# Inverting and gating the sums of two softmaxes together, in a two-layer decoder trunk

## Chip, cores and metric

The kernel runs on one core of a Trainium2 chip. The metric is the device time of one execution, in microseconds; the median of three runs of the kernel before is 620.65 us (620.62 to 620.73). Engines: PE is TensorE (PEld its weight loads), DVE is VectorE, ACT is ScalarE, POOL is GpSimd, SP is SyncE, which issues the DMAs.

## The reference

Two layers work on x of 256 tokens by 1024 columns, in float32. Each has an attention part and an MLP, both between RMS norms.

The attention part projects the normed x to 2848 columns. Eight heads are *gated* (called nsa): each has a compressed, a selected and a window branch. With 256 tokens, all four blocks of 64 are selected and the window covers every earlier key, so the selected and the window branch are two causal softmaxes over different keys and values. Their outputs are added with a sigmoid gate per token, head and branch. Eight other heads are *forgetting* (called fox): one causal softmax each, with a learned decay added to the scores.

```python
g = jax.nn.sigmoid(gate_logits + gate_bias)
o = g[..., 0:1] * o_cmp + g[..., 1:2] * o_sel + g[..., 2:3] * o_win    # per gated head
p = softmax(q @ k.T * scale + cum_q - cum_k, causal)                   # per forgetting head
x = x + rms_norm(concat([o_nsa, o_fox]) @ w_out, g_post_mix)
x = x + rms_norm(square(relu(rms_norm(x, g_pre_mlp) @ w_up)) @ w_down, g_post_mlp)
```

## The kernel before

**Tiles.** Tokens are cut in two halves of 128 (t = 0, 1). Every weight tile (512 KB mostly) is loaded by SP into wraw and split on chip into a rounded high part whi (an ACT copy) and the rest wlo (a DVE subtraction); a product is three matmuls, high by high, high by low, low by high. Seven whi and seven wlo tiles and nine raw ones rotate.

**Who sets the order.** The code doesn't issue instructions. It records them in a `Recorder`, which then plans the order on every engine: `schedule` (line 303) is a list scheduler that knows a cost for each operation (`_cost`, line 453), a latency between engines (`_latency`, line 430) and how many buffers each tag has; among the instructions that are ready it takes the one with the lowest rank. `order` (line 288) plans once by the recorded order and then four times more with due times worked back from the plan for PE (`deadlines`, line 260), and keeps the plan that ends first. So a change in what is recorded can move instructions on all engines. On the chip each engine then runs its own list in order and waits on semaphores. All recorded instructions carry line 411 in the profile, so one goes by tile names there.

**The attention stage.** A list `flat` has 24 entries per layer: for each of four pairs of gated heads, par = 0, 1 and branch br = 1, 2; then, for each of four pairs of forgetting heads, par = 0, 1. The loop at line 1378 walks it as a pipeline, entry i in the step i: in step i it records the scaling of entry i - 1, the scores and exponentials of entry i, and the transposes of entry i - 2; three entries behind, where a group of heads is complete, the products with the values (`pv`, line 1283). Between these it records pieces of the projections and of the output projection (`fill`, line 1198), so that PE has other matmuls while a softmax is under way.

For one entry, with 384 score columns (128 for t = 0, 256 for t = 1):

- `scores` (line 1231): PE writes scores to PSUM; for each t, DVE adds mask or decay, stores minus the scaled scores to the tile pr and their minimum to st[:, t]; ACT takes the exponential in place and puts its sum into st[:, 2 + t]. Both branches of a gated head come from one set of score matmuls (`nsa_scores`), both heads of a forgetting pair from another (`fox_scores`).
- `scale` (line 1253): DVE inverts the two sums with one reciprocal and multiplies pr, for each t, by the inverse; for a gated branch the same instruction multiplies by the gate too, as a second scalar operand.
- `probs_T` (line 1264): PE transposes pr in three blocks to PSUM, ACT copies that to prT (or, for odd pairs of gated heads, to a larger tile prX).

There are three pr tiles, four st tiles (128x4) and six prT tiles.

**The end of the stage.** The outputs (oT) are multiplied by w_out into four PSUM accumulators, x for t = 0 and acc for t = 1; the last four row blocks need the forgetting heads (`out_last`, line 1418). Then, for each t, `sandwich` (line 727) squares and sums on ACT, makes the new normed rows mg on DVE, PE turns mg (`to_xT`, line 710), and ACT and DVE split the turned rows into high and low parts of xT, with which the MLP's matmuls start.

Of the kernel before, what the change touches and what calls it, by code (L numbers as in the profile page):

```python
# [20 lines left out]
AF = mybir.ActivationFunctionType  # L21
OP = mybir.AluOpType
PSUM = bass.MemoryType.PSUM

P = 128
# [32 lines left out]
SEGS = ((0, 128, 0), (128, 384, 1))  # L58
# [474 lines left out]
def trunk(nc, A, consts_in, out, sbp, pp, dram):  # L533
    def tile(shape, dtype, name, tag=None, bufs=1):
        return nc.tile(sbp[(tag or name) not in OPERANDS], shape, dtype, name, tag, bufs)

    def psum(tag):
        return nc.tile(pp, [P, 512], F32, tag, tag, {"acc": 2, "x": 2, "s": 3, "o": 1}[tag], psum=True)

    def small(shape, name, bufs=2):  # L540
        return tile(shape, F32, name=name, tag=name, bufs=bufs)
# [17 lines left out]
    for l in range(DEPTH):  # L559
        at = 0  # L560
        for c, (a, b) in enumerate(CHUNKS):
# [3 lines left out]
            for q, (k0, k1) in enumerate(parts_of(l, c)):  # L565
# [4 lines left out]
                if (c, q) in RIDES:  # L570
                    s, j = RIDES[c, q]
# [39 lines left out]
    for k in range(8):  # L611
        if k in (2, 3):
            f = both[:, k - 2]
        elif k < 2:
            f = tile([P, D], F32, name="first", tag="raw", bufs=RBUFS)
        else:
            f = tile([P, D], F32, name="first", tag=f"act{k % 2}", bufs=2)
        o = 0 if k else 8
        f = f[:, 0:o + NFIRST]
        a = 8 + k * NFIRST - o  # L620
# [19 lines left out]
    ps = psum("o")  # L640
# [13 lines left out]
    def load_gains(*rows):  # L654
        g = tile([P, 2, D], F32, name="gains", tag="gain")
        for i, (name, l) in enumerate(rows):
            nc.sync.dma_start(g[:, i, :], A[name][l].partition_broadcast(P))
        return [g[:, i, :] for i in range(2)]
# [141 lines left out]
    for l in range(DEPTH):  # L800
# [6 lines left out]
        par = {} if first else dict(zip(("smT", "bias", "w2"), params))  # L807
        kv_tok, kS, kW, q_tok, q_rot = ([None] * 2 for _ in range(5))
        vS, vW, fV, gate = ([None] * 2 for _ in range(4))
        gates = small([P, NT, 24], "gate")  # L810
        T = {}
# [238 lines left out]
        def forget_bias(pair):  # L1050

            b = tile([P, 2, 384], F32, name="bias", tag="raw", bufs=RBUFS)
            nc.sync.dma_start(b, T["cum"][2 * pair:2 * pair + 2, :].partition_broadcast(P))
            for o in (0, 2 * P):
                nc.gpsimd.affine_select(out=b[:, :, o:o + P], in_=b[:, :, o:o + P], pattern=[[0, 2], [-1, P]],
                                        compare_op=OP.is_ge, fill=NEG, base=0, channel_multiplier=1)
            T["fb", pair] = b
# [140 lines left out]
        def fill(n):  # L1198
            for _ in range(n):
                if step() in ("wait", "end"):  # L1200
                    return
# [6 lines left out]
        def fox_scores(pair):  # L1208

            ps = [psum("s") for _ in range(2)]  # L1210
            rows = [slice(par * HD, par * HD + HD) for par in range(2)]
            with nc.stretch():
                for o, n, q0 in ((0, 128, 0), (128, 256, 128)):
                    for par, h in enumerate(rows):
                        nc.tensor.matmul(ps[par][:, o:o + n], T["fqT"][h, pair, q0:q0 + P], T["fkT"][h, pair, 0:n],
                                         start=o == 0, stop=o > 0, skip_group_check=True)
            return [(x[:, 0:128], x[:, 128:384]) for x in ps]

        def nsa_scores(e):

            pair, par = e[1:3]
            g = pair // 2
            q = T["qS"][:, 2 * pair + par, :]
            ps = [psum("s"), psum("x")]
            for t, n in ((0, P), (1, S)):
                for j in range(2):
                    nc.tensor.matmul(ps[t][:, :2 * n].rearrange("p (b n) -> p b n", b=2), q[:, t * P:t * P + P],
                                     kx[j][:, g, :, 0:n], start=j == 0, stop=j == 1)
            return [(ps[0][:, br * P:br * P + P], ps[1][:, br * S:br * S + S]) for br in range(2)]

        def scores(e):
            kind, pair, par, br = e[:4]
            if kind == "fox":
                if par == 0:
                    T["sc"] = fox_scores(pair)
                ps = T["sc"][par]
            else:
                if br == 1:
                    T["sc"] = nsa_scores(e)
                ps = T["sc"][br - 1]  # L1240
            p = small([P, 384], "pr", 3)
            st = small([P, 4], "st", 4)
            for a, b, t in SEGS:
                nc.vector.tensor_tensor_reduce(
                    out=p[:, a:b], in0=ps[t], in1=T["fb", pair][:, par, a:b] if kind == "fox" else
                    cst[:, C_MASK + 256 - (b - a):C_MASK + 256], op0=OP.add, op1=OP.min,
                    scale=-0.125, scalar=3.0e38, accum_out=st[:, t:t + 1])
            for a, b, t in SEGS:
                nc.scalar.activation(p[:, a:b], p[:, a:b], AF.Exp, scale=-1.0, bias=st[:, t:t + 1],
                                     accum_out=st[:, 2 + t:3 + t])  # L1250
            return p, st

        def scale(e, p, st):
            kind, pair, par, br = e[:4]
            nc.vector.reciprocal(st[:, 2:4], st[:, 2:4])
            for a, b, t in SEGS:
                if kind == "fox":
                    nc.vector.tensor_scalar(p[:, a:b], p[:, a:b], st[:, 2 + t:3 + t], None, op0=OP.mult)
                else:
                    c = 3 * (2 * pair + par) + br  # L1260
                    nc.vector.tensor_scalar(p[:, a:b], p[:, a:b], st[:, 2 + t:3 + t], gate[t][:, c:c + 1],
                                            op0=OP.mult, op1=OP.mult)

        def probs_T(p, eng, e):
            ps = psum("s")
            with nc.stretch():
                for a in (0, 128, 256):
                    nc.tensor.transpose(ps[:, a:a + P], p[:, a:a + P], ident)
            kind, pair, par, br = e
            if kind == "nsa" and pair % 2:  # L1270

                if br == 1:
                    T["prX"] = tile([P, 4, S], F32, name="prX", tag=f"act{par}", bufs=2).rearrange("p b n -> p (b n)")
                pT = T["prX"][:, (br - 1) * 384:br * 384]
            else:
                pT = small([P, 384], "prT", 6)
            if eng:
                nc.scalar.activation(pT, ps[:, :384], AF.Copy)
            else:
                nc.vector.tensor_copy(pT, ps[:, :384])  # L1280
            return pT
# [87 lines left out]
        flat = [("nsa", pair, par, br) for pair in range(4) for par in range(2) for br in (1, 2)]  # L1369
# [4 lines left out]
        st = {}  # L1374
# [1 line left out]
        o = None  # L1376
        nc.lane = len(nc.ops)
        for i in range(len(flat) + 4):
            if 0 <= i - 1 < len(flat):
                scale(flat[i - 1], *st[i - 1])  # L1380
            if i < len(flat):
                if 14 <= i < 22 and i % 2 == 0:
                    forget_bias(i // 2 - 7)
                st[i] = scores(flat[i])
                if i == 15:
                    done.add("nsa")
                    g_post, g_pre2 = load_gains(("g_post_mix", l), ("g_pre_mlp", l))
            fill(1)
            if i in side:
                side[i]()  # L1390
                fill(1)
            if 0 <= i - 2 < len(flat):
                pTs[flat[i - 2]] = probs_T(st.pop(i - 2)[0], 1, flat[i - 2])
            fill(1)
            j = i - 3
            if 0 <= j < len(flat) and flat[j][2] == 1 and flat[j][3] != 1:
                kind, pair, par, br = flat[j]
                if pair % 2:
                    o = psum("o")
                    if br:  # L1400
                        nc.tensor.matmul(o, T["vbig"][:, pair // 2], T["pcT"][pair // 2], start=True, stop=False,
                                         skip_group_check=True)
                    cols = lambda q: [(q // 2) * HD] * 2 if br else [2 * q * HD, 2 * q * HD + HD]
                    pv(o, [[([pTs.pop((kind, q, x, b)) for x in range(2)], (fV, vS, vW)[b], cols(q))
                            for b in ((1, 2) if br else (0,))] for q in (pair - 1, pair)], not br)
                    o_evac(o, kind, pair)
            if i >= 12 or i % 2:
                fill(1)
# [207 lines left out]
```

## Time and profile before

| | |
|---|---|
| median of the runs | 620.65 us |
| the profiled execution | 620.53 us, of it 618.4 us in the span of the trace |
| mean granted TensorE clock | 0.997 |
| instructions in the trace | 9854 |
| ACT's exponentials of pr | 96 |
| the first scaling of pr starts, the last one | 62.2 us, 419.9 us |

The profile is of one execution. Busy shares are of the span. A row of the view of groups gives the engine, the operation, out<-in by tile names with shapes, a count, the busy time with the mean duration of one in ns, and then the engine's idle time just before them with what ended it. A row of the view in order of time gives start and length in us, and a count of merged instructions; start to start of neighbours is what an engine needs for one, since the end of an instruction overlaps with the next. A row of the view of waits gives who waited for whom, the total, the number of times and the longest.

### The profile page before, as it was taken

The page shows a single profiled execution, that of the slowest core. Times are in us where ns is not written, and L with a number is a line of the kernel's source. Part 1 is how long each engine was busy: PE and PEld are TensorE (multiplying, and loading weights), DVE is VectorE, ACT ScalarE, POOL GpSimd, SP SyncE. Part 2 cuts the span into 40 slices and gives each one's busy share as a digit, 9 for nine tenths or more (in the row PEclk, how much of TensorE's full clock was granted, in tenths as well). Part 3 has the DMA queues.
Part 4 walks back from the last instruction along what each step waited for, and adds up shares of the span by engine and source line. Part 5 has one row for each costly group of instructions (what it writes and reads, how often), then busy time and mean ns, then how long its engine had stood idle before and what let it go on. Part 6 is the DMA issues. An engine that isn't in the chain of part 4 may idle for free.

```text
span 618.4 us, 9854 instructions
## 1 busy us (share of the span) xinstructions
PE 611.0 (99%) x3494; PEld 514.6 (83%) x3494; DVE 465.3 (75%) x1021; ACT 388.9 (63%) x760; POOL 10.8 (2%) x20
## 2 busy tenths in 40 slices
PE   9999999999999999999999999999999999999995
PEld 7989987788888888888888888778888888888884
DVE  6889998689966567557598999886996575566534
ACT  7766788567655555545466769775776456456522
POOL 0001200000000000000000020000000000000000
PEclk9999999999999999999999999999999999999998
DMA  8996746519765565564346781653386665666001
GB/s 323 401 355 209 268 137 223 171 36 307 254 191 191 182 205 196 184 197 140 107 137 239 265 312 71 204 205 104 131 299 203 191 197 175 200 197 181 32 0 68
DMA packets 34817, 118.86 MB, mean 192 GB/s; under 512 B 4144, under 2 KB 4304, under 8 KB 34768
## 3 DMA queue, kind: packets, MB, share of 16 engines
q1 hardware_dynamic: 34768, 118.23, 57.5%
q8 instruction: 27, 0.44, 0.3%
q14 instruction: 22, 0.18, 0.1%
HBM read 117.15 MB, written 1.07 MB: 191 GB/s over the span
## 4 chain that ended last, share of the span: by engine, by line
PE 99%; DVE 0%; DVEq 0%; issue 0%; ACT 0%
PE s L411 35%; PE acc L411 31%; PE x L411 25%; PE o L411 7%; DVE x L411 0%; DVE m L411 0%; DVEq L1612 0%; DVE rsqrt L411 0%; ACT rl L411 0%
## 5 line engine op out<-in xcount | busy, mean ns | idle before, releaser
L411 DVE TENSOR_TENSOR wlo<-wraw,whi 128x1024 fp32r<-128x1024 f32 (+1 forms) x188 | 225.5, 1201 | 97.9 <-ACT whi L411 57.9
L411 ACT ACTIVATE whi<-wraw 128x1024 fp32r<-128x1024 f32 (+1 forms) x188 | 195.4, 1042 | 108.2 <-PE acc L411 72.9
L411 PE MATMUL s<-xT,whi 128*128 128x512 f32 x448 | 106.5, 390 | 0.0
L411 PEld LDWEIGHTS s<-xT,whi 128*128 128x128 f32 x448 | 83.4, 188 | 16.8
L411 PE MATMUL x<-whi,aT 128*128 128x512 f32 x256 | 88.6, 391 | 0.0
L411 PE MATMUL acc<-whi,aT 128*128 128x512 f32 x256 | 88.4, 390 | 0.0
L411 PEld LDWEIGHTS s<-xT,wlo 128*128 128x128 f32 x448 | 57.4, 191 | 2.2
L411 PE MATMUL s<-xT,wlo 128*128 128x256 f32 x448 | 58.1, 283 | 0.0
L411 PEld LDWEIGHTS acc<-whi,aT 128*128 128x128 f32 x256 | 48.0, 188 | 10.0
L411 PEld LDWEIGHTS x<-whi,aT 128*128 128x128 f32 x256 | 48.1, 188 | 9.6
L411 PE MATMUL x<-wlo,aT 128*128 128x512 f32 x128 | 50.0, 390 | 0.0
L411 PE MATMUL acc<-wlo,aT 128*128 128x512 f32 x128 | 49.9, 390 | 0.0
L411 ACT ACTIVATE pr<-pr,st 128x256 f32<-128x256 f32 (+1 forms) x96 | 42.8, 449 | 5.8 <-DVE st L411 5.5
L411 PE MATMUL acc<-xT,whi 128*128 128x256 f32 (+1 forms) x192 | 42.4, 324 | 0.0
L411 PE MATMUL acc<-whi,xT 128*128 128x512 f32 (+1 forms) x128 | 37.2, 354 | 0.0
L411 PE MATMUL x<-whi,xT 128*128 128x512 f32 x112 | 35.7, 395 | 0.1
L411 PEld LDWEIGHTS acc<-xT,whi 128*128 128x128 f32 x192 | 31.7, 190 | 3.3 <-issue 0.8
L411 ACT ACTIVATE h<-s 128x256 f32<-128x256 f32 x56 | 21.2, 378 | 16.0 <-PE s L411 16.0
L411 ACT ACTIVATE rl<-h 128x512 f32<-128x512 f32 x28 | 17.7, 633 | 18.0 <-DVE h L411 18.0
L411 PE MATMUL acc<-xT,wlo 128*128 128x256 f32 x128 | 28.6, 286 | 0.0
L411 ACT ACTIVATE rl<-x 128x512 f32<-128x512 f32 x24 | 14.6, 610 | 22.2 <-PE x L411 18.0
L411 PEld LDWEIGHTS acc<-wlo,aT 128*128 128x128 f32 x128 | 24.0, 188 | 5.0
(220 smaller groups left out, 963.6 us busy)
## 6 DMA issues: line engine op xcount, KB each, us to landing
wraw<-in_w_up_dram SPq DMA_DIRECT2D x64, 512.0 KB, 4.0
wraw<-in_w_down_dram SPq DMA_DIRECT2D x64, 512.0 KB, 3.7
wraw<-in_w_in_dram SPq DMA_DIRECT2D x36, 512.0 KB, 4.9
wraw<-in_w_out_dram SPq DMA_DIRECT2D x16, 512.0 KB, 5.6
w<-in_cmp_w_k_dram SPq DMA_DIRECT2D x8, 512.0 KB, 4.9
w<-in_cmp_w_v_dram SPq DMA_DIRECT2D x8, 512.0 KB, 4.6
bias<-sums SPq DMA_DIRECT2D x8, 384.0 KB, 6.1
first<-in_first_dram SPq DMA_DIRECT2D x7, 384.0 KB, 5.2
```

The costliest lines, as they stand in the source:

```text
L411: getattr(getattr(self.nc, op.engine), name)(*[real(v) for v in args], **{k: real(v) for k, v in kw.items()})
```

## The change

Entries are scaled two at a time: both branches of a gated head, or both heads of a forgetting pair. They share one tile st of eight columns, whose columns 4 to 7 hold the four sums. One reciprocal inverts the four; for a gated head one small multiplication brings in the four gates (two branches, two t); each of the four scalings then has a single scalar operand. In the loop nothing is scaled in odd steps, and both entries in the next even one, so the first entry of a pair is scaled one step later than before, in the step in which its transposes are recorded. There are four pr tiles in place of three, two st tiles of twice the size in place of four, and five prT tiles in place of six.

```diff
-            p = small([P, 384], "pr", 3)
-            st = small([P, 4], "st", 4)
+            p = small([P, 384], "pr", 4)
+
+            j = 2 * (par if kind == "fox" else br - 1)
+            if j == 0:
+                T["st"] = small([P, 8], "st", 2)
+            st = T["st"]
             for a, b, t in SEGS:
                 nc.vector.tensor_tensor_reduce(
...
-                    scale=-0.125, scalar=3.0e38, accum_out=st[:, t:t + 1])
+                    scale=-0.125, scalar=3.0e38, accum_out=st[:, j + t:j + t + 1])
             for a, b, t in SEGS:
-                nc.scalar.activation(p[:, a:b], p[:, a:b], AF.Exp, scale=-1.0, bias=st[:, t:t + 1],
-                                     accum_out=st[:, 2 + t:3 + t])
+                nc.scalar.activation(p[:, a:b], p[:, a:b], AF.Exp, scale=-1.0, bias=st[:, j + t:j + t + 1],
+                                     accum_out=st[:, 4 + j + t:5 + j + t])
             return p, st
 
-        def scale(e, p, st):
+        def scale(e, ps, st):
             kind, pair, par, br = e[:4]
-            nc.vector.reciprocal(st[:, 2:4], st[:, 2:4])
-            for a, b, t in SEGS:
-                if kind == "fox":
-                    nc.vector.tensor_scalar(p[:, a:b], p[:, a:b], st[:, 2 + t:3 + t], None, op0=OP.mult)
-                else:
-                    c = 3 * (2 * pair + par) + br
-                    nc.vector.tensor_scalar(p[:, a:b], p[:, a:b], st[:, 2 + t:3 + t], gate[t][:, c:c + 1],
-                                            op0=OP.mult, op1=OP.mult)
+            f = st[:, 4:8]
+            nc.vector.reciprocal(f, f)
+            if kind == "nsa":
+                c = 3 * (2 * pair + par) + 1
+                f = f.rearrange("p (b t) -> p b t", b=2)
+                nc.vector.tensor_mul(f, f, gates[:, :, c:c + 2].rearrange("p t b -> p b t"))
+            for j, p in enumerate(ps):
+                for a, b, t in SEGS:
+                    x = st[:, 4 + 2 * j + t:5 + 2 * j + t]
+                    nc.vector.tensor_scalar(p[:, a:b], p[:, a:b], x, None, op0=OP.mult)
...
-                pT = small([P, 384], "prT", 6)
+                pT = small([P, 384], "prT", 5)
...
-            if 0 <= i - 1 < len(flat):
-                scale(flat[i - 1], *st[i - 1])
+            if 0 <= i - 1 < len(flat) and (i - 1) % 2:
+                scale(flat[i - 1], (st[i - 2][0], st[i - 1][0]), st[i - 1][1])
```

## The prediction, made before the changed kernel was run

> **What bounds the kernel now.** I read the page first (busy shares, the 40 slices, the chain that ended last), then who waited for whom on the TensorE, then the order of its matmuls in time where the two attention stages run.
>
> ```profile
> span 618.4 us, 9854 instructions
> ...
> PE 611.0 (99%) x3494; PEld 514.6 (83%) x3494; DVE 465.3 (75%) x1021; ACT 388.9 (63%) x760; POOL 10.8 (2%) x20
> ...
> PE   9999999999999999999999999999999999999995
> ...
> DVE  6889998689966567557598999886996575566534
> ...
> PE 99%; DVE 0%; DVEq 0%; issue 0%; ACT 0%
> ```
>
> ```profile
> PE o L411 <- PEq L1606: 0.8, 1, 0.8
> ```
>
> PE is busy in every slice but the last, 99% of the chain is PE, and the one wait that the view of waits has for PE is 0.8 us at the start. VectorE is nearly full in slices 4 to 8 and 24 to 28, where the attention stages lie, but nothing in the chain is waiting for it. Busy PE need not be PE at its pace, so I look at starts. Near the end of the first layer's attention:
>
> ```profile
> 115.91 0.49 PE L411 MATMUL s<-cst,pr 128*128 128x128 f32 x3
> 116.16 0.47 PE L411 MATMUL acc<-whi,oT 128*128 128x512 f32 x1
> 116.47 0.39 PE L411 MATMUL x<-whi,oT 128*128 128x512 f32 x1
> 116.70 0.40 PE L411 MATMUL x<-wlo,oT 128*128 128x512 f32 x1
> ```
>
> A 512-wide matmul is followed by the next after 0.23 us (116.47 to 116.70). Behind a group of probability transposes (s<-cst,pr) the first matmul is followed after 0.31 us (116.16 to 116.47). These 0.08 us of leaving an f32 group are the only irregularity that I find among the starts of the 128x128 matmuls in the two attention stages; none stands noticeably late behind a softmax. So before has hardly a stall that a faster softmax could remove.
>
> **The Trainium skill, weighed.** "Perfetto Trace Analysis", section "Identifying the Most-Contended Engine", says that matmul busy share is a poor measure of how near TensorE is to its limit and that the weight-load share is the better one. That is 83% here, so by this rule PE has room. The trace answers with a stretch of the MLP and the two attention stretches:
>
> ```profile
> 52.00:128.00 76.00, 76.00 (x544) 62.01 (x543) 66.88 (x236) 55.57 (x160) 5.97 (x8) 1.00 0.56 185
> 364.00:428.00 64.00, 64.00 (x416) 50.89 (x415) 55.78 (x204) 48.15 (x143) 2.71 (x6) 1.00 0.52 182
> 550.00:560.00 10.00, 10.00 (x46) 8.28 (x45) 4.81 (x4) 4.25 (x4) 0.00 (x0) 1.00 0.57 202
> ```
>
> (Columns: stretch, length, then PE, weight loads, VectorE, ScalarE, GpSimd, the granted clock, DMA.) In the MLP, where VectorE is half idle and can delay nothing, the weight loads also fill 8.28 of 10 us; in attention 62.01 of 76 (82%) and 50.89 of 64 (80%). The share of 83% is therefore the stream at full pace, not room. I go by the row, and keep the rule as the rival on the fast side.
>
> **The change, part by part.** The durations of the VectorE work it touches:
>
> ```profile
> L411 DVE TENSOR_SCALAR pr<-pr,st,gate 128x256 f32<-128x256 f32 x32 | 13.2, 411 | 0.2
> ...
> L411 DVE TENSOR_SCALAR pr<-pr,st,gate 128x128 f32<-128x128 f32 x32 | 11.1, 346 | 0.0
> ...
> L411 DVE RECIPROCAL st<-st 128x2 f32<-128x2 f32 x48 | 7.4, 157 | 2.6 <-ACT pr L411 2.3
> ```
>
> ```profile
> L411 DVE TENSOR_SCALAR pr<-pr,st 128x256 f32<-128x256 f32 x16 | 5.6, 349 | 0.2
> ...
> L411 DVE TENSOR_SCALAR pr<-pr,st 128x128 f32<-128x128 f32 x16 | 4.5, 280 | 0.0
> ```
>
> ```profile
> 97.70 1.22 DVE L411 TENSOR_TENSOR wlo<-wraw,whi 128x1024 fp32r<-128x1024 f32 x1
> 98.84 0.16 DVE L411 RECIPROCAL st<-st 128x2 f32<-128x2 f32 x1
> 98.91 1.21 DVE L411 TENSOR_TENSOR xo<-x,gains 128x1024 f32<-128x1024 f32 x1
> ```
>
> ```profile
> 66.08 0.17 DVE L411 TENSOR_TENSOR csm<-csm,gate 128x16 f32<-128x16 f32 x1
> 66.16 0.16 DVE L411 RECIPROCAL st<-st 128x2 f32<-128x2 f32 x1
> ```
>
> 1. *Scalings with one scalar.* 64 scalings of gated branches lose the gate operand and become what the forget heads already have: 411 to 349 ns (32 of them) and 346 to 280 ns (32). 32 x 62 + 32 x 66 ns = 4.1 us of VectorE, over both layers.
> 2. *Half the reciprocals.* 48 become 24. One lasts 157 ns, but the next instruction starts 0.07 us later (98.84 to 98.91), so 24 fewer free about 24 x 0.07 = 1.7 us of queue. The wider one (128x4) I take at the same price.
> 3. *A small multiplication by the gates*, 16 of them. The trace has none of 128x4; the nearest is the 128x16 one at 66.08, whose successor starts 0.08 us later: 16 x 0.08 = 1.3 us. Bounds: 0.07 (the reciprocal's step) and 0.17 us (its whole duration, if the next must wait for it).
>
> VectorE thus gets 4.1 + 1.7 - 1.3 = 4.5 us, 2.2 per layer, of 66.88 and 55.78 busy us. None of it is on the path: PE hides all of it, since it waits for VectorE nowhere. What is given up is nothing either, as long as PE has matmuls to put in between.
>
> 4. *The added wait.* The first softmax of a pair now waits until the second one's sums are there. Behind the pair's reciprocal stand, on VectorE's in-order queue, the next pair's maxima and the weight splits, and PE's transposes wait for the scalings. One more softmax on ScalarE takes, from its first exponential to the next task,
>
> ```profile
> 105.53 0.51 ACT L411 ACTIVATE pr<-pr,st 128x256 f32<-128x256 f32 x1 [1.21 <-DVE st L411]
> ...
> 106.49 1.06 ACT L411 ACTIVATE whi<-wraw 128x1024 fp32r<-128x1024 f32 x1
> ```
>
> 106.49 - 105.53 = 0.96 us for its two exponentials. So the first transposes of a pair come about 1 us later after their scores. In the two programs' instruction orders I counted the matmuls between a pair's last scores and its first transposes, at the steps seen above: in before the shortest cover that this gives is an estimated 3.6 us (for one softmax), in after 4.1 us (for a pair); most are 5 to 8 us. The planner has moved other matmuls into the longer gap, and it has them: projections, then the output projection, in both layers. Cost taken: 0. Where the cover is gone the cost is the overshoot, below.
>
> 5. *Buffers* (three pr become four, six prT five, st tiles shared): they only alter when the planner lets things start. SP's queue loads the same tiles, one small load a place later; no transfer is on the chain. Cost 0.
>
> 6. *The order that comes out.* Both programs issue the same matmuls. By kind (64-row scores, 64-column products, transposes, the rest) PE's stream changes kind 197 times before and 199 times after: one group more, 0.08 us. The place that I can see getting worse is the end of each attention stage. In before, between the second turning of mg and the first matmul with xT, PE has seven matmuls left:
>
> ```profile
> 431.88 0.60 PE L411 MATMUL s<-cst,mg 128*128 128x128 f32 x4
> 432.24 0.71 PE L411 MATMUL acc<-whi,oT 128*128 128x512 f32 x2
> 432.78 0.40 PE L411 MATMUL acc<-wlo,oT 128*128 128x512 f32 x1
> ...
> 433.94 0.39 PE L411 MATMUL s<-whi,xT 128*128 128x512 f32 x1
> ```
>
> ```profile
> 432.15 1.06 ACT L411 ACTIVATE xT<-s 128x512 fp32r<-128x512 f32 x2
> ```
>
> ```profile
> 432.76 1.29 DVE L411 TENSOR_TENSOR xT<-s,xT 128x512 fp32r<-128x512 f32 x2 [0.50 <-ACT xT L411]
> ```
>
> In after there are two, in both layers, because the last pair's products come later and five of them are used up as cover there. Laid on these rows, the first xT matmul would stand at 432.78 instead of 433.94, and the third, which needs the low half, at 432.78 + 2 x 0.23 = 433.24. The first low half is ready at 432.76 + 1.29 / 2 = 433.4 or a little later. That is a wait of about 0.2 us per layer (none if the copy, held up here by a weight split, starts earlier; 0.5 if two splits stand before it): 2 x 0.2 = 0.4 us.
>
> The sum is made against the profiled execution's own 620.53 us (618.4 of span and 2.1 around it; the median of the runs is 620.65, 0.12 above): 620.53 + 0 (VectorE's gain) + 0.08 + 0.4 = **621.0 us**.
>
> **The rivals.** *A, slower: the pair's wait runs past its cover.* The shortest chain of a pair is two softmaxes on ScalarE (1.9 us) and the maxima, reciprocal, scalings and hand-overs around them, by the rows above and estimated latencies some 3.7 us, against the tightest cover of 4.1. One weight split (step 1.14 us, from 97.70 to 98.84) in VectorE's queue at the wrong moment overshoots by 0.7 us. From two such per layer on, this decides: 4 x 0.7 + 0.5 = 3.3, so 623.8 us; with one per layer 622.4. For it: VectorE is 88% busy there (66.88 of 76.00 us). Against it: as tight chains in before show no late matmul. "Perfetto Trace Analysis", section "Optimizing Scalar/DVE Operations", speaks for it: where an unsaturated VectorE makes bubbles on others, instructions should be broken up, and this change merges them; no bubble in before bears it out.
>
> *B, faster: PE has room after all*, and VectorE's 4.5 us come off where its queue paces the stage. At most 616.0 us; with half of it real, 618.3. Against it: the even starts and the 0.8 us of PE waits. The skill's weight-load rule above would have it so.
>
> *C, the change doesn't do what it says*: the single-scalar form or the wide reciprocal costs as much as before. VectorE then gains nothing, and since that is hidden, the time is that of the forecast.
>
> **How the numbers follow.** About 0.2% (1.2 us) is what a measurement of this kernel can tell from no change. Forecast with C: 76%, its own range 620.4 to 621.7. A: 19%, of which a third is beyond 622.4. B: 5%. All of the forecast's own range lies within 0.2%, A beyond it above, B beyond it below: faster 0.05, same 0.76, slower 0.19. The range leaves out B and the far end of A: 620.3 to 622.4 us.
>
> **What would show it.** In the changed kernel's profile: scalings at about 349 and 280 ns, 24 reciprocals, VectorE's busy time down by some 4 to 8 us (with durations, not steps), PE's still 611 and the span at 618.9; a pitch of 0.23 us through attention; a short gap ahead of the third xT matmul in each layer. I am wrong if waits of PE for pr or for prT appear in the view of waits, with matmuls behind transposes later than 0.31 us, or if the span falls by more than 1 us, which would need idle time on PE that I have not seen.

## The result, and the profile after

The changed kernel takes 621.63 us (median of 22 runs, 621.18 to 622.27), the kernel before 620.76 us in the same session (22 runs, 620.55 to 621.36). The ratio is 1.0013, with a 95% interval of 1.0007 to 1.0018: 0.87 us slower, a difference clear of the noise but inside the 0.2% that the prediction takes for no change. The forecast was 621.0 us, within a range of 620.3 to 622.4. The profiled execution took 621.62 us, 1.09 above the 620.53 of before's.

The page of the changed kernel, the lines that answer to those of before (span, busy shares, slices of PE and of VectorE, the chain that ended last), and the view of PE's waits:

```profile
span 619.5 us, 9847 instructions
...
PE 612.0 (99%) x3494; PEld 514.4 (83%) x3494; DVE 461.6 (75%) x1013; ACT 389.6 (63%) x760; POOL 9.6 (2%) x20
...
PE   9999999999999999999999999999999999999995
...
DVE  6889988689976567556598999786996575566534
...
PE 99%; DVE 0%; DVEq 0%; issue 0%; ACT 0%
```

```profile
PE o L411 <- PEq L1612: 0.8, 1, 0.8
```

VectorE has 3.7 us less to do and PE is busy 1.0 us longer with the same 3494 matmuls. On the page little else has moved (ScalarE is busy 0.7 us longer): PE's only wait is the same 0.8 us. VectorE's groups (operation, tiles and shapes, count, busy us, mean ns) show that the instructions became what was intended:

```profile
L411 DVE TENSOR_SCALAR pr<-pr,st 128x256 f32<-128x256 f32 x48 | 16.7, 347 | 0.3
...
L411 DVE TENSOR_SCALAR pr<-pr,st 128x128 f32<-128x128 f32 x48 | 13.6, 283 | 0.0
...
L411 DVE RECIPROCAL st<-st 128x4 f32<-128x4 f32 x24 | 4.1, 171 | 3.7 <-ACT pr L411 3.7
...
L411 DVE TENSOR_TENSOR st<-st,gate 128x4 f32<-128x4 f32 x16 | 2.5, 156 | 0.1
```

The two attention stretches (the columns are those of the prediction's table) have 3.1 and 1.9 us less of VectorE, 63.75 and 53.93 in place of 66.88 and 55.78, and PE fills them as before:

```profile
52.00:128.00 76.00, 76.00 (x542) 61.91 (x541) 63.75 (x230) 55.41 (x160) 4.52 (x8) 1.00 0.59 188
364.00:428.00 64.00, 64.00 (x416) 50.55 (x415) 53.93 (x198) 47.99 (x142) 4.28 (x7) 1.00 0.57 187
```

So where is PE's microsecond? The view of waits has PE's weight loads too (PEld: who waited for whom, total, times, longest). Several of its rows are new in the changed kernel, and one of them names a tile from the end of the attention stage, once in each layer:

```profile
PEld s L411 <- DVE xT L411: 0.7, 2, 0.3
```

Its total counts a weight load's normal idle time as well, so I go to the matmuls in order of time there, in the first layer:

```profile
129.56 0.60 PE L411 MATMUL s<-cst,mg 128*128 128x128 f32 x4
129.92 0.48 PE L411 MATMUL acc<-wlo,oT 128*128 128x512 f32 x1
130.23 0.39 PE L411 MATMUL acc<-whi,oT 128*128 128x512 f32 x1
130.46 0.40 PE L411 MATMUL s<-whi,xT 128*128 128x512 f32 x1
130.70 0.39 PE L411 MATMUL s<-wlo,xT 128*128 128x512 f32 x1
130.99 0.74 PE L411 MATMUL s<-whi,xT 128*128 128x512 f32 x2
131.57 0.40 PE L411 MATMUL s<-wlo,xT 128*128 128x512 f32 x1
```

This is the wait that was foretold: two matmuls behind the second turning of mg, and the third xT matmul starts 0.29 us after the second instead of 0.23. The two that are merged at 130.99 take 0.58 to the next in place of 0.46: the matmul behind a wait comes 0.11 us late as well. The wait is 0.07 us before rounding, and with the late matmul it costs 0.07 + 0.11 = 0.18 us, in both layers.

The second place the prediction had not seen, and no view of waits lists it: the idle time is too short. Only the distances of the starts show it, where PE comes from the products of the gated heads with their values (second group):

```profile
104.75 0.87 PE L411 MATMUL s<-cst,pr 128*128 128x128 f32 x6
105.52 0.50 PE L411 MATMUL x<-whi,oT 128*128 128x512 f32 x1
105.85 0.40 PE L411 MATMUL x<-wlo,oT 128*128 128x512 f32 x1
```

```profile
104.87 0.60 ACT L411 ACTIVATE oT<-o 128x512 fp32r<-128x512 f32 x1 [0.55 <-PE o L411]
```

ScalarE's copy of the new oT ends at 104.87 + 0.60 = 105.47, and the output projection's matmul that needs it starts at 105.52. At the same place in before, PE has a product with an older part of oT behind the six transposes:

```profile
101.98 0.87 PE L411 MATMUL s<-cst,pr 128*128 128x128 f32 x6
102.61 0.47 PE L411 MATMUL x<-wlo,oT 128*128 128x512 f32 x1
102.92 0.63 PE L411 MATMUL x<-whi,oT 128*128 128x512 f32 x2
```

```profile
102.10 0.60 ACT L411 ACTIVATE oT<-o 128x512 fp32r<-128x512 f32 x1
```

The product at 102.61 starts before the copy there ends (102.70), so it doesn't need it. 101.98 to 102.61 is 0.63 us, 104.75 to 105.52 is 0.77; with a late restart of 0.02 that is 0.16 us, again in both layers (the second place is the matmul at 409.84 us).

**One account for all kernels.** To compare orders I took, for every three neighbouring matmuls by kind (128x512, 128x256, transposes, 64-row scores and so on), the median start-to-start time in the profiles of before and after. Summed over a kernel's own order, less the sum for before, that is its column *groups*: what the order would cost with no waits. The column *waits* is the sum of all single intervals that are over 0.03 us above their median (transposes of the projections left out, whose kinds I did not separate). *First 41* is the start of the 41st matmul, up to which all kernels have the same order. *Rest* is what is then left of the start of the last matmul, against before's (all from the profiled executions, us). The first number is the median against the median of before in the same session.

| kernel | median against before | groups | waits | first 41 | rest |
|---|---|---|---|---|---|
| before | | 0 | 0.00 | 12.01 | 0 |
| changed | +0.87 | -0.19 | 0.76 | 12.28 | +0.18 |
| changed, again (e12) | +0.68 | -0.19 | 0.63 | 12.15 | +0.09 |
| e1 single scalar alone | +0.31 | +0.23 | 0.00 | 12.53 | -0.04 |
| e2 pairs alone | -0.08 | -0.66 | 0.37 | 12.14 | +0.04 |
| e3 pairs for gated heads | -0.03 | -0.71 | 0.28 | 12.04 | +0.21 |
| e4 low half later | +0.30 | -0.19 | 0.27 | 12.11 | +0.13 |
| e5 low half first | +1.60 | -0.19 | 1.58 | 12.14 | +0.06 |
| e6 the same, before | 0.00 | 0.00 | 0.00 | 12.05 | +0.05 |
| e7 no scaling | +0.30 | -0.45 | 0.56 | 12.08 | +0.21 |
| e8 gate apart | +4.05 | +0.25 | 3.66 | 11.91 | +0.18 |
| e9 changed, other prices | +0.54 | -0.70 | 0.81 | 12.46 | +0.21 |
| e10 before, other prices | +0.36 | -0.02 | 0.32 | 12.66 | +0.15 |
| e11 e3, other prices | +0.16 | -0.94 | 0.78 | 12.14 | +0.14 |

The columns *first 41* and *waits* are read from single starts. *Groups* and *rest* are softer: they depend on how finely the kinds are told apart. With other divisions of the same starts (the output tile added to the kind, two neighbours in place of three, the interval at another place among the three) the groups of the changed kernel come out between -0.34 and +0.04, and those of e2 between -0.7 and 0.0; *rest* moves the other way. So a group cost of some tenths is an estimate whose sign is not sure in the changed kernel.

For the changed kernel, without the column *groups*: from the 41st matmul to the last, PE takes 599.44 us in before and 600.19 in the changed kernel, 0.75 more (0.53 in e12). Four waits come in both of its profiles (2 x 0.18 at the tail and 2 x 0.14 for oT, whose restart of 0.02 is under the threshold: the 0.63 of the second profile). They are about what the two profiles lose; groups and many small differences make up the rest, one way or the other, and the start comes on top.

### The profile page after: what moved, and what is told of

Same layout as the page of the kernel before. It is cut to its first block, busy times and chain, and to the rows that moved or that the text cites. A ratio compares the mean times of both kernels' runs of the same rounds, so it can differ in the third digit from the quotient of the medians.

```text
span 619.5 us, 9847 instructions
## 1 busy us (share of the span) xinstructions
PE 612.0 (99%) x3494; PEld 514.4 (83%) x3494; DVE 461.6 (75%) x1013; ACT 389.6 (63%) x760; POOL 9.6 (2%) x20
## 4 chain that ended last, share of the span: by engine, by line
PE 99%; DVE 0%; DVEq 0%; issue 0%; ACT 0%
PE s L411 35%; PE acc L411 31%; PE x L411 25%; PE o L411 7%; DVE x L411 0%; DVE m L411 0%; DVEq L1618 0%; DVE rsqrt L411 0%; ACT rl L411 0%
```

## The experiments

The medians are of 10 or 11 runs (e8: 5), and the interval of such a ratio is about 0.09% either way, 0.55 us. A step of 0.3 us can't rest on one such number; so each run is read by its median and by its trace.

Three theories were told apart. *Order*: PE is the bound, VectorE's time is worth nothing, and only the order of PE's matmuls, with the short waits it brings, moves the time. *Pair*: the wait of a pair's first softmax for the second costs, whatever the order. *VectorE*: its time is on the path.

**e1: the single scalar alone.** From the kernel before:

```diff
             nc.vector.reciprocal(st[:, 2:4], st[:, 2:4])
+            if kind == "nsa":
+                c = 3 * (2 * pair + par) + br
+                nc.vector.tensor_mul(st[:, 2:4], st[:, 2:4], gates[:, :, c])
             for a, b, t in SEGS:
...
+                nc.vector.tensor_scalar(p[:, a:b], p[:, a:b], st[:, 2 + t:3 + t], None, op0=OP.mult)
```

> One part alone: every scaling has a single scalar, each entry keeps its own reciprocal (128x2) and gets its own small multiplication by its two gates; the step, the waits and the buffers are those of before. Order theory (TensorE is the bound; only the order of its matmuls, and the short waits that this order brings with it, move the time): the tail has six or seven matmuls behind the second turning of mg as in before, and laid on the starts measured in before and after, the groups of this kernel's order cost 0.2 us more; 620.8 to 621.1. Pair theory (the first softmax's wait for the second is what costs, wherever the matmuls stand): nothing is paired, so the time of before, 620.7 to 620.9. VectorE theory (its time is on the path): scalings save 4.1 us and the 32 small multiplications cost 32 x 0.08 = 2.6, so 1.5 us less, 619.3.

Measured: 620.94 against 620.63 us, ratio 1.0005 (0.9996 to 1.0013). The scalings did get shorter (349 and 284 ns), but the 32 small multiplications last 163 ns each, and VectorE's busy time is 464.9 us, only 0.4 under before's where 1.5 was expected. So the run hardly tests the VectorE theory: its 619.3 fails because the saving wasn't there. No wait appears; by the account the groups cost 0.23 more, which is not sure. Order and pair can't be separated by it.

**e2: pairs alone, two scalars as before.** From the changed kernel, the small multiplication goes and the gate comes back into the scaling:

```diff
-                f = f.rearrange("p (b t) -> p b t", b=2)
-                nc.vector.tensor_mul(f, f, gates[:, :, c:c + 2].rearrange("p t b -> p b t"))
...
+                        nc.vector.tensor_scalar(p[:, a:b], p[:, a:b], x, gates[:, t, c:c + 1], op0=OP.mult, op1=OP.mult)
```

> The other part alone: pairs with one reciprocal, the later step and the buffers of the change, but each gated scaling keeps its gate as a second scalar and there is no small multiplication. Order theory: in this kernel's order the tail has seven matmuls behind the second turning of mg again, the first product with a freshly copied oT comes later than in the changed kernel, and more of the 64-wide groups stand beside each other (0.2 us for each that is joined): 0.4 to 0.7 us under before, 620.0 to 620.4, although all pairs wait. Pair theory: the wait is the whole change, so the time of the changed kernel, 621.5 to 621.8. VectorE theory: 24 reciprocals less, 1.7 us, so 619.0.

Measured: 620.55 against 620.63, ratio 0.9998 (0.9989 to 1.0007). All pairs wait as in the changed kernel, with the same buffers, and the loss is not there; the pair theory's 621.6 lies outside the interval (621.1 at most), and so does the VectorE theory's 619.0 (VectorE's busy time fell to 463.0 us). Nor did the kernel gain 0.4, so the order theory's 620.0 to 620.4 was missed as well: of its waits 0.30 us lie at 18 and 316 us, where no other profile has any and no softmax runs. Without them its profile would end 0.4 under before's; that is one execution.

**e3: pairs for the gated heads only.** The forgetting entries get their own reciprocal, one step earlier, as in before.

```diff
-            if 0 <= i - 1 < len(flat) and (i - 1) % 2:
-                scale(flat[i - 1], (st[i - 2][0], st[i - 1][0]), st[i - 1][1])
+            if 0 <= i - 1 < len(flat):
+                if flat[i - 1][0] == "fox":
+                    scale(flat[i - 1], (st[i - 1][0],), st[i - 1][1])
+                elif (i - 1) % 2:
+                    scale(flat[i - 1], (st[i - 2][0], st[i - 1][0]), st[i - 1][1])
```

> The change for gated heads alone: each forgetting entry is scaled on its own, one step earlier, as in before (with four st tiles); all other things as in the changed kernel. Order theory: the tail has its seven matmuls, the 64-wide groups are joined more often (0.7 us under before by the starts measured in the two kernels), but the first product with a freshly copied oT comes as soon as in the changed kernel and waits 0.16 us for it in each layer: 620.76 - 0.7 + 0.3 = 620.4, between 620.2 and 620.7. Pair theory: 8 of 12 pairs are left in each layer, so two thirds of the 0.87 us of the change: 621.3. VectorE theory: near the full 4.5 us, 616.5.

Measured: 620.60 against 620.63, ratio 0.9996 (0.9987 to 1.0004), within the order theory's range at its slow end; the pair theory's 621.3 and the VectorE theory's 616.5 lie outside the interval. The tail's wait is gone, the 0.14 us wait for oT stands ahead of the matmuls at 105.3 and 409.0 us as in the changed kernel.

**e4: the low half later.** In the changed kernel the two matmuls with xT's low half for row blocks 0 and 1 come behind the four with the high half.

```diff
+                    if t == 0 and k < 2:
+                        for v in range(2):
+                            nc.tensor.matmul(ps, xT[0][:, k, 0:P], w[v][:, k % 2, :], start=k + v == 0, stop=False)
+                        if k == 1:
+                            for z in range(2):
+                                nc.tensor.matmul(ps, xT[1][:, z, 0:P], w[0][:, z, :], start=False, stop=False)
+                        continue
                     mm3(ps, [y[:, k, t * P:t * P + P] for y in xT[:2]], [y[:, k % 2, :] for y in w], k == 0, k == 7)
```

> The changed kernel, but where the MLP starts, the two matmuls that need the low half of xT (row blocks 0 and 1, first token half) come behind the four that need the high half; the order up to there is the same. Order theory: the wait ahead of the third xT matmul and the late one behind it (0.07 + 0.11 us in each layer) go, nothing else changes: 621.63 - 0.36 = 621.3. Pair theory, with the cost made inside the attention stage: 621.6, no change. If the time of the tail was only the pair's delay moved to where it shows, the gap moves to the next matmul that needs something late and the time stays at 621.6.

Measured: 620.93 against 620.63, ratio 1.0003 (0.9994 to 1.0012). PE at the tail:

```profile
130.06 0.39 PE L411 MATMUL acc<-whi,oT 128*128 128x512 f32 x1
130.29 0.40 PE L411 MATMUL s<-whi,xT 128*128 128x512 f32 x1
130.53 0.39 PE L411 MATMUL s<-wlo,xT 128*128 128x512 f32 x1
130.76 0.40 PE L411 MATMUL s<-whi,xT 128*128 128x512 f32 x1
130.99 0.39 PE L411 MATMUL s<-wlo,xT 128*128 128x512 f32 x1
131.22 0.84 PE L411 MATMUL s<-whi,xT 128*128 128x512 f32 x3
```

An even 0.23 us: the wait is gone and does not come back at a later matmul. The waits in the account fall from 0.63 to 0.27 (the two for oT), by the 0.36 that was expected.

**e5 and e6: the same wait made larger, in both kernels.** The matmul with the low half comes first:

```diff
+                    if t == 0 and k == 0:
+                        for j, (u, v) in enumerate(((1, 0), (0, 0), (0, 1))):
+                            nc.tensor.matmul(ps, xT[u][:, k, 0:P], w[v][:, 0, :], start=j == 0, stop=False)
+                        continue
                     mm3(ps, [y[:, k, t * P:t * P + P] for y in xT[:2]], [y[:, k % 2, :] for y in w], k == 0, k == 7)
```

> The changed kernel, with the suspected wait made larger: of the first three matmuls with xT in the MLP (row block 0, first token half), the one that needs the low half of xT comes first instead of third. The order up to there is the same, two matmuls stand behind the second turning of mg. Order theory: in the changed kernel the low half was ready for a matmul at 130.99 us, and the first xT matmul stood at 130.46, so the first one now waits 0.53 us and restarts 0.11 late, 0.64 us in place of 0.18 per layer: 621.6 + 2 x 0.46 = 622.6 (622.3 to 622.9). Pair theory (the cost lies in the attention stage): 621.6, unchanged.

> The same edit in the kernel before, where seven matmuls stand behind the second turning of mg. Order theory: the first xT matmul stands at 433.94 us there and the first low half is ready at 433.4 to 433.6, so the cover holds and the time is that of before, 620.6 to 620.9; the same edit is worth 0.9 us in one kernel and nothing in the other. If instead the low half itself were late in any order, this one would lose as much as the other, 621.6.

Measured: the changed kernel 622.27 against 620.67, ratio 1.0025 (1.0016 to 1.0034), just under the range given; the kernel before 620.67 against 620.67, ratio 1.0000 (0.9991 to 1.0009). The tail of the changed kernel, then of the other:

```profile
130.12 0.40 PE L411 MATMUL acc<-whi,oT 128*128 128x512 f32 x1
130.88 0.74 PE L411 MATMUL s<-whi,xT 128*128 128x512 f32 x2 [0.37 <-DVE xT L411]
131.46 0.40 PE L411 MATMUL s<-wlo,xT 128*128 128x512 f32 x1
```

```profile
129.81 0.39 PE L411 MATMUL acc<-whi,oT 128*128 128x512 f32 x1
130.04 0.62 PE L411 MATMUL s<-whi,xT 128*128 128x512 f32 x2
130.49 0.39 PE L411 MATMUL s<-wlo,xT 128*128 128x512 f32 x1
```

130.12 to 130.88 is 0.76 in place of 0.23: a wait of 0.53 and 0.12 of restart. The waits grow by 1.58 - 0.63 = 0.95 us (0.92 expected). The same edit costs nothing where seven matmuls stand ahead. This shows the tail's cover as a cause, with its price.

**e7: no scaling.** This kernel leaves out the inverse, the gate and the scaling of pr.

```diff
-            if 0 <= i - 1 < len(flat) and (i - 1) % 2:
+            if False:
                 scale(flat[i - 1], (st[i - 2][0], st[i - 1][0]), st[i - 1][1])
```

> The changed kernel without the scaling at all: no inverse, no gate, no scaling of pr, so the softmaxes are neither normalized nor gated (this part of the computation is left out). That takes some 33 us from VectorE (48 x 0.349 + 48 x 0.280 + the small ones), and the pair's wait and one hand-over out of each chain. Order theory: TensorE is the bound, so VectorE's time is worth nothing; in this order the tail has seven matmuls and no product comes soon behind a copy of oT, and the groups cost 0.3 us less than in before: 620.1 to 620.9. Pair theory: no wait is left, the time of before or a little under, 620.2 to 620.8 (it does not tell these two apart). VectorE theory: if only a quarter of the 33 us were on the path, 613; if half, 605.

Measured: 620.97 against 620.67, ratio 1.0006 (0.9997 to 1.0015). From its page:

```profile
PE 611.4 (99%) x3494; PEld 514.7 (83%) x3494; DVE 437.0 (71%) x877; ACT 389.0 (63%) x760; POOL 10.6 (2%) x20
```

VectorE has 28.3 us less to do than in before (24.6 less than in the changed kernel, where some 33 were expected), and the time isn't lower; it is 0.07 over the order theory's range. This shows that VectorE's time in these stages is hidden, to within the half microsecond of the interval, and it refutes the VectorE theory. (Its 0.56 us of waits lie at other places, 0.4 of them at scores that come early, with kx and qS, at 70.1 and 374.4 us.)

**e8: the gate apart.** The kernel before, with each gated scaling as two instructions:

```diff
-                    nc.vector.tensor_scalar(p[:, a:b], p[:, a:b], st[:, 2 + t:3 + t], gate[t][:, c:c + 1],
-                                            op0=OP.mult, op1=OP.mult)
+                    nc.vector.tensor_scalar(p[:, a:b], p[:, a:b], st[:, 2 + t:3 + t], None, op0=OP.mult)
+                    nc.vector.tensor_scalar(p[:, a:b], p[:, a:b], gate[t][:, c:c + 1], None, op0=OP.mult)
```

> The kernel before with more VectorE work and nothing paired: each gated scaling becomes two, one by the inverse and one by the gate, each with a single scalar: 64 instructions more, 32 x (2 x 0.349 - 0.411) + 32 x (2 x 0.280 - 0.346) = 16 us of VectorE, 8 us in each layer, whose attention stage it fills to some 95% and more. Order theory: the planner answers with an order that uses up the tail's matmuls as cover (none stands behind the second turning of mg) and that has the first product close behind the copy of oT: groups +0.1, oT 2 x 0.16, the tail 2 x (0.18 + 2 x 0.23) = 1.3, so 622.4 (621.9 to 623); no transposes wait long. VectorE theory: the 16 us come on top, 636. Pair theory: nothing is paired, 620.7. Stalls behind softmaxes, if VectorE has no room left, would come on top: over 623.

Measured: 624.72 against 620.67, ratio 1.0064 (1.0052 to 1.0077). The mechanism is the one expected and its size is not (4.05 us for 1.7). VectorE's busy time is 475.0 us, 9.7 more than before's where 16 were expected; no transpose of pr waits over 0.1 us. Of the waits, 0.53 and 0.14 us are for the copy of oT, and about 0.2 lie at the eight scores at 101.01 us, which take 1.01 us in place of 0.85. The rest of the loss, 1.4 us in each layer, is at the tail, where no matmul is left between the turnings of mg and the first with xT:

```profile
129.75 0.39 PE L411 MATMUL acc<-whi,oT 128*128 128x512 f32 x1
130.22 1.63 PE L411 MATMUL s<-cst,mg 128*128 128x128 f32 x8
131.75 0.50 PE L411 MATMUL s<-whi,xT 128*128 128x512 f32 x1
132.08 0.40 PE L411 MATMUL s<-wlo,xT 128*128 128x512 f32 x1
132.67 0.73 PE L411 MATMUL s<-whi,xT 128*128 128x512 f32 x2 [0.19 <-DVE rsqrt L411]
```

The turnings start late, eight of them take 1.53 us to the next matmul (four take 0.36 above), and the third xT matmul comes 0.59 us after the second. I had priced the last wait alone, not those for mg, and not the longer one for oT.

**e9 to e12: the same instructions in another order.** Only the planner's two prices for a change of tile shape differ, in the changed kernel (e9), in before (e10) and in e3 (e11); e12 is the changed kernel as it is.

```diff
-ENTER, LEAVE = 90, 200
+ENTER, LEAVE = 200, 300
```

> The changed kernel's own instructions, all of them, in another order: only the two prices that the planner uses for a change of tile shape on TensorE are other (200 and 300 ns in place of 90 and 200). In the order that comes out, seven matmuls stand behind the second turning of mg in both layers, the first product that needs the new oT comes 0.94 us behind the products with the values instead of 0.63, and by the starts measured in before and after the groups cost 0.7 us less than in before. Order theory: the change's loss goes and a little more, 620.0 to 620.4, with no gap at the tail and none ahead of the first product with oT. Pair theory: the pairs wait as in the changed kernel, so its time, 621.6.

> The kernel before with the same two prices: seven matmuls in the tail, groups 0.0 us against before. Order theory: the time of before, 620.5 to 620.9; so the setting alone is worth nothing, and what the run with the changed kernel gains by it is the loss that its first order had. If the setting alone makes a better kernel, this one gains as much as that one, 620.0.

> The version that the runs point to: pairs for the gated heads alone, with the same two prices: the fewest groups of all (0.9 us less than in before by the measured starts), seven matmuls in the tail, the product with the new oT 0.94 us behind. Order theory: 619.8 to 620.3, under before and under the changed kernel. Pair theory: 621.3 as for the other order of this version. VectorE theory: no more than the other order of this version.

> The changed kernel unaltered, for a comparison on the same chip with the same instructions in the other order. All theories: 621.4 to 621.8, and the same two gaps in each layer, 0.16 us ahead of the first product with oT and 0.18 us at the tail.

Measured against 620.70 us: e9 621.24, ratio 1.0009 (1.0000 to 1.0018); e10 621.06, 1.0002 (0.9993 to 1.0011); e11 620.86, 1.0002 (0.9993 to 1.0011); e12 621.38, 1.0009 (1.0000 to 1.0018). My expectations of e9 and e11 failed, by 0.8 and 0.6 us, and e10 lies 0.16 above its range. In e9 and e11 the orders are those that were counted (groups -0.70 and -0.94 by the account, which is no measurement of these runs) and the tail has no wait, but other waits took their place, 0.81 and 0.78 us; in e11 0.63 of them lie at the product with the new oT. In e9, PE and ScalarE at the place of the oT copy:

```profile
104.85 0.87 PE L411 MATMUL s<-cst,pr 128*128 128x128 f32 x6
105.48 0.48 PE L411 MATMUL acc<-whi,oT 128*128 128x512 f32 x1
105.83 0.50 PE L411 MATMUL x<-whi,oT 128*128 128x512 f32 x1
106.17 0.40 PE L411 MATMUL x<-wlo,oT 128*128 128x512 f32 x1
```

```profile
104.70 0.51 ACT L411 ACTIVATE pr<-pr,st 128x256 f32<-128x256 f32 x1
...
105.20 0.58 ACT L411 ACTIVATE oT<-o 128x512 fp32r<-128x512 f32 x1
```

One matmul more stands ahead of the product with the new oT, but the copy now starts 0.35 us behind the first transpose (0.12 in the changed kernel), held up by an exponential of the next pair, and ends at 105.78: the product waits all the same (0.15 us in the first layer, 0.18 in the second, with the restart). Transposes of pr come 0.10 us late at 112.6 and 416.6 us as well; in e10, where nothing is paired, such transposes wait 0.23 us. So the distance in matmuls on PE was not enough to foretell a wait: the start on ScalarE, in its queue, decides as much. No version that I ran is measurably faster than the kernel before.

## Why the prediction was right, and where it was not

*What bounds the kernel* held: e7 takes 28 us off VectorE and gains nothing, and the weight-load share is 83% on its page and on the changed kernel's alike. Rival B fell with that. The Trainium skill names this share, beside MFU, which was not worked out here, as the measure of TensorE's headroom ("Perfetto Trace Analysis", section "Identifying the Most-Contended Engine"); read alone, its 83% promises room that no run here found. The Trainium skill's advice to break up instructions that cause bubbles on other engines ("Perfetto Trace Analysis", section "Optimizing Scalar/DVE Operations") has no bubble behind a softmax to work on here, in before or after: the wide reciprocals of e2 cost nothing.

*Steps 1 to 3* held: 347 and 283 ns for 349 and 280, 24 reciprocals, 16 small multiplications of 156 ns. By durations that is 4.1 + (48 x 0.157 - 24 x 0.171) - 16 x 0.156 = 5.0 us, as much as the two attention stretches lost; over the whole span VectorE's busy time fell by 3.7, a little less than the 4 to 8 I named, since instructions that the change doesn't touch took about 1 us longer in this execution.

*Step 4* (the pair's wait costs nothing where there is cover) held in its first half: no transpose waits for a pair in the changed kernel, rival A's mechanism doesn't appear, and e2 pairs everything at the time of before. It failed in "the planner has moved other matmuls into the longer gap, and it has them: cost taken 0". I looked only at the gap between scores and transposes. A matmul that is moved there is missing elsewhere, and I asked where for the tail alone; ahead of the first product with the second copy of oT cover is missing too, 0.16 us per layer. That is the failed term: 0 in the sum, 0.32 us measured. That it was the longer gap that took this cover is argued, not shown.

*Step 5* (buffers) held: e2 has the changed buffers.

*Step 6*: the tail's wait, 0.2 us per layer in the sum, measured 0.18, and shown by e4 to e6. That the size fits is in part luck: the wait itself is 0.07 us, where the prediction's rows gave 0.16, and the other 0.11 is the late matmul behind it, which the sum didn't have. The 0.08 us for a kind change was wrong. The rows at 129.56 to 130.23 tell why: four transposes take 0.36 us and the matmul behind them 0.31, 0.67 together; at 0.11 for a transpose (three take 0.25 in the prediction's row at 115.91, four 0.36) and 0.23 for the matmul they would take 0.67 anyway. Only the last transpose's time moves to the matmul behind it. What the new order's groups cost in all stays open within some tenths; the account says 0.19 us less, not 0.08 more.

*The sum.* The direction was right and 621.0 was 0.63 below the median. Of that 0.23 is the base: 620.53 is a low execution of the kernel before (the medians of its four sessions are 620.63 to 620.76). The other 0.4 is the step itself, 0.48 forecast and 0.87 measured: 0.32 for the waits for oT, which the sum didn't have, less 0.04 at the tail, and 0.1 of groups and small differences that I can't separate. The profile lies further off (PE 612.0 and a span of 619.5 for 611 and 618.9), since it also began 0.26 us later over 40 identical matmuls.

What stays open: why the planner's search ends in an order with two matmuls in the tail for the changed kernel and with seven for e2, which pairs the same softmaxes with slower scalings. That the pairs, by their later transposes, use up the cover is argued from the order, and e8 shows it for transposes that are later through a slower VectorE. e2 shows that pairing need not do it. The wait for oT was seen wherever the order has that distance and the copy that start (changed, e3, e4, e5, e12) and not where it doesn't (before, e2, e6), but no run took it away alone; so the tail's 0.36 us is shown by experiment, and the 0.32 for oT is read from the traces. The order theory explains more than it foretold: its ranges held or nearly held in e1 and e3 to e7, and were missed in e2 and e8 to e11, by up to 1.7 us, each time through waits that a count of matmuls didn't show.

## What to carry to other kernels

Where one engine is the bound and an automatic order fills its gaps, a change on another engine can be paid in order and not in work, as here: look at every place where the bound engine waits for a fresh result (ends of stages, the first use of a copy), and ask what stood there as cover before and after. Count that cover in time up to the producer's own start in its queue, not in instructions on the bound engine. And before making an engine faster, take its work out altogether once: here that single run (e7) would have said that no saving on VectorE could be worth more than some tenths of a microsecond.

## What the runs showed of the hardware

A matmul between two groups of other tile shapes was dear. In before, one stands between the 64-row scores and the products with values at this place; in e3 the groups touch:

```profile
404.19 0.93 PE L411 MATMUL s<-fkT,fqT 64*128 64x128 f32 x8
405.04 0.51 PE L411 MATMUL acc<-wlo,oT 128*128 128x512 f32 x1
405.48 0.87 PE L411 MATMUL o<-prT,vS 128*64 128x256 f32 x8
```

```profile
404.64 0.93 PE L411 MATMUL s<-fkT,fqT 64*128 64x128 f32 x8
405.49 0.87 PE L411 MATMUL o<-prT,vS 128*64 128x256 f32 x8
```

The scores take 0.85 us in both; the matmul between takes 0.44 instead of 0.23, so joining these two groups saves 0.21 us if the matmul takes 0.23 where it stands instead.

A matmul behind a wait is followed late: 0.11 to 0.12 us at the tail, whether the wait was 0.07 (changed kernel) or 0.53 us (e5).

The start of the program varies: up to the 41st matmul, in the same order in all kernels, 11.91 to 12.66 us pass. Profiles whose kernels have the same order for much longer lie closer together (12.11 to 12.28 in the changed kernel, e12, e4 and e5; 12.01 and 12.05 in before and e6), so whether the rest belongs to the execution or to the kernel is not shown. The 42nd in the profile of before and in that of e10:

```profile
12.24 0.39 PE L411 MATMUL x<-wlo,xT 128*128 128x512 f32 x1
```

```profile
12.89 0.39 PE L411 MATMUL x<-wlo,xT 128*128 128x512 f32 x1
```

The two differ by 0.65 us, more than most of the edits here are worth, which is a reason to compare two profiles from their first common matmul on.
